# Relu and row mean on one core: 126 rows a partition between two blocks of 128 rows, and the last block's means stored turned, as four runs behind the main store

## The chip, the cores and the metric

The kernel runs on one core of one Trainium2 chip. The time is the device time of one execution in microseconds (us); medians are over several executions. A profile is a separate look at one execution, and its span is about 1.4 us shorter than the execution's time (161.59 us and 160.2 us for the profiled run of the kernel before).

In the text, DVE is VectorE, ACT is ScalarE, POOL is GpSimd and SP is SyncE, which issues the DMAs here.

## The reference

```python
batch, seq, dim = 32, 512, 1024
x = np.random.randn(batch, seq, dim).astype(np.float32)

def reference(x):
    relu_x = np.maximum(x, 0)
    return np.mean(relu_x, axis=-1).astype(np.float32)
```

These are 16,384 rows of 1024 numbers: 67.11 MB are read, 65,536 bytes written.

## The kernel before

The first 128 rows lie one to a partition. They are loaded ahead of all else, and their means are turned by a 32x32 transpose into four rows of 32, which are stored in mid-stream. The other 16,256 rows lie 127 to a partition (`J` after the subtraction): seven loads of 16 rows, then 7, 4, 2 and 1 rows, then the last row in pieces of columns. ACT and DVE take rows in turn; each pass is a relu with a running sum.

```python
xfirst, xmain = xf[:P, :], xf[P:, :]
outfirst, outmain = out.flatten()[:P], out.flatten()[P:]
J = J - 1
xr = xmain.rearrange("(p j) d -> p j d", p=P, j=J)
...
row_pieces = [7, 4, 2, 1]
col_pieces = [512, 256, 256]
...                      # the last row: ACT takes piece 1, DVE piece 2
nc.scalar.wait_ge(loaded[i + 1], 16)
act_row(nc, last[:, :512], last[:, D:D + 1]).then_inc(act, 1)
nc.vector.wait_ge(loaded[i + 2], 16)
dve_row(nc, last[:, 512:768], last[:, D + 1:D + 2]).then_inc(dve, 1)
nc.vector.wait_ge(act, n_done + 1)
nc.vector.wait_ge(dve, n_done + 1)
nc.vector.wait_ge(loaded[i + 3], 16)
nc.vector.scalar_tensor_tensor(      # piece 3, and the two sums that lie behind it
    out=last[:, 768:], in0=last[:, 768:], scalar=0.0, in1=scale[:, :], op0=ALU.max, op1=ALU.mult,
    accum_out=res[:, J - 1:J],
).then_inc(dve, 1)

nc.sync.wait_ge(pool, 2)
nc.sync.wait_ge(dve, n_done + 2)
nc.sync.dma_start(out=outr, in_=res[:, :]).then_inc(stored, 16)
```

The two partial sums of the last row lie in the columns right behind it, so the last instruction on DVE (called the **combining instruction** below) reduces the third piece and adds them in one go. The one store of 128 runs of 508 B follows it.

Of the kernel before, what the change touches and what calls it, by code (L numbers as in the profile page):

```python
# [8 lines left out]
ALU = mybir.AluOpType  # L9
# [3 lines left out]
def act_row(nc, src, acc):  # L13

    return nc.scalar.activation(out=src, in_=src, func=ACT.Relu, accum_out=acc)  # L15


def dve_row(nc, src, acc, init=None):

    return nc.vector.tensor_scalar(  # L20
        out=src, in0=src, scalar1=0.0, scalar2=init,
        op0=ALU.max, op1=ALU.add, accum_out=acc,
    )


def issue_ahead_of_entry_barrier(nc, n):


    entry = nc.cur_f.blocks[0].instructions
    for _ in range(n):  # L30
        body, load = next(
            (block.instructions, k)
            for block in nc.cur_f.blocks[1:]
            for k, ins in enumerate(block.instructions)
            if ins.opcode == "DMACopy"
        )
        first = body[load]
        assert first.engine == mybir.EngineType.SP and not first.sync_info.on_wait
        assert all(i.opcode in ("Drain", "EventSemaphore") or i.engine != first.engine for i in body[:load])
        del body[load]  # L40
        at = next(k for k, i in enumerate(entry) if i.engine == first.engine and i.opcode == "Drain")
        entry.insert(at, first)


@with_exitstack
def kernel(
    ctx: ExitStack,
    tc: tile.TileContext,
    x: bass.AP,
    out: bass.AP,  # L50
):


    tc.close()
    tc.compile()  # L55

    nc = tc.nc
    P = nc.NUM_PARTITIONS
    xf = x.flatten_outer_dims()
    R, D = xf.shape  # L60
    assert R % P == 0
    J = R // P
    inv = 1.0 / D

    xfirst, xmain = xf[:P, :], xf[P:, :]
    outfirst, outmain = out.flatten()[:P], out.flatten()[P:]
    J = J - 1
    xr = xmain.rearrange("(p j) d -> p j d", p=P, j=J)
    outr = outmain.rearrange("(p j) -> p j", p=P, j=J)

    NB = 16
    BUFS = 3
    full = J // NB

    row_pieces = [7, 4, 2, 1]
    assert full * NB + sum(row_pieces) + 1 == J
    col_pieces = [512, 256, 256]
    assert sum(col_pieces) == D

    def sbuf(name, *shape):  # L80
        return ctx.enter_context(nc.sbuf_tensor(name, list(shape), F32))

    bufs = [sbuf(f"rows{b}", P, NB, D) for b in range(BUFS)]
    sums, res, part = sbuf("sums", P, J), sbuf("res", P, J), sbuf("part", P, 2)


    last = sbuf("last", P, D + 2)
    scale = sbuf("scale", P, D // 4 + 2)

    row0, mean0, turned0 = sbuf("row0", P, D), sbuf("mean0", P, 32), sbuf("turned0", P, 32)  # L90


    loaded = [nc.alloc_semaphore(f"loaded{i}") for i in range(full + len(row_pieces) + len(col_pieces) + 1)]
    act, dve, pool = (nc.alloc_semaphore(n) for n in ("act", "dve", "pool"))
    first = nc.alloc_semaphore("first")
    stored = nc.alloc_semaphore("stored")



    hinted = (nc.scalar, nc.vector)  # L100
    flag = nc.alloc_registers("flag", engines=[e.engine for e in hinted])
    nc.regs_mov(flag, 1)
    nc.br("rows_begin", engines=mybir.ALL_ENGINES)
    body = ctx.enter_context(nc.body("rows_begin", valid_engines=mybir.ALL_ENGINES))
    hints = [e.mark_branch_hint_location() for e in hinted]


    def load(i, dst, src):
        nc.sync.dma_start(out=dst, in_=src).then_inc(loaded[i], 16)

    def buf_free(t):

        if t >= BUFS:
            nc.sync.wait_ge(act, t - BUFS + 1)
            nc.sync.wait_ge(dve, t - BUFS + 1)

    for t in range(full):
        buf_free(t)
        if t == 0:
            load(-1, row0[:, :], xfirst)  # L120
        load(t, bufs[t % BUFS][:, :, :], xr[:, t * NB:(t + 1) * NB, :])
        if t == BUFS:

            nc.sync.wait_ge(first, 2)
            nc.sync.dma_start(
                out=outfirst.rearrange("(q i) -> q i", i=32), in_=turned0[0:P:32, :],
            ).then_inc(stored, 16)
    j0 = full * NB
    buf_free(full)
    xt = bufs[full % BUFS]  # L130
    lo, i = 0, full
    for n in row_pieces:
        load(i, xt[:, lo:lo + n, :], xr[:, j0 + lo:j0 + lo + n, :])
        lo, i = lo + n, i + 1
    c = 0
    for w in col_pieces:
        load(i, last[:, c:c + w], xr[:, J - 1, c:c + w])
        c, i = c + w, i + 1


    nc.gpsimd.memset(mean0[:, :], 0.0)  # L141
    nc.gpsimd.memset(scale[:, :], inv).then_inc(pool, 1)  # L142

    def rows(i, xt, lo, n, j0):
        nc.scalar.wait_ge(loaded[i], 16)
        nc.vector.wait_ge(loaded[i], 16)
        for k in range(lo, lo + n):
            j = j0 + k
            done = (dve_row if j % 2 else act_row)(nc, xt[:, k, :], sums[:, j:j + 1])
            if k >= lo + n - 2:  # L150
                done.then_inc(dve if j % 2 else act, 1)

    def finish(after, lo, hi):

        nc.gpsimd.wait_ge(act, after)
        nc.gpsimd.wait_ge(dve, after)
        nc.gpsimd.tensor_scalar(  # L157
            out=res[:, lo:hi], in0=sums[:, lo:hi], scalar1=inv, scalar2=0.0, op0=ALU.mult, op1=ALU.add,
        )

    nc.scalar.wait_ge(pool, 1)
    nc.vector.wait_ge(pool, 1)
    nc.scalar.wait_ge(loaded[-1], 16)
    nc.scalar.activation(  # L164
        out=row0[:, :], in_=row0[:, :], func=ACT.Relu, scale=inv, accum_out=mean0[:, 0:1],
    ).then_inc(first, 1)
    nc.vector.wait_ge(first, 1)
    nc.vector.transpose(turned0[:, :], mean0[:, :]).then_inc(first, 1)  # L168
    for t in range(full):
        rows(t, bufs[t % BUFS], 0, NB, t * NB)  # L170
    finish(full, 0, j0)
    lo, i = 0, full
    for n in row_pieces[:-1]:
        rows(i, xt, lo, n, j0)
        lo, i = lo + n, i + 1
    finish(i, j0, j0 + lo)


    prev = xt[:, lo, :]
    nc.scalar.wait_ge(loaded[i], 16)  # L180
    act_row(nc, prev[:, :448], part[:, 0:1]).then_inc(act, 1)
    nc.vector.wait_ge(loaded[i], 16)
    dve_row(nc, prev[:, 448:], part[:, 1:2]).then_inc(dve, 1)
    n_done = i + 1
    nc.gpsimd.wait_ge(act, n_done)
    nc.gpsimd.wait_ge(dve, n_done)
    nc.gpsimd.tensor_scalar(  # L187
        out=res[:, J - 2:J - 1], in0=part[:, 0:1], scalar1=part[:, 1:2], scalar2=inv, op0=ALU.add, op1=ALU.mult,
    ).then_inc(pool, 1)
    nc.scalar.wait_ge(loaded[i + 1], 16)  # L190
    act_row(nc, last[:, :512], last[:, D:D + 1]).then_inc(act, 1)
    nc.vector.wait_ge(loaded[i + 2], 16)
    dve_row(nc, last[:, 512:768], last[:, D + 1:D + 2]).then_inc(dve, 1)
    nc.vector.wait_ge(act, n_done + 1)
    nc.vector.wait_ge(dve, n_done + 1)
    nc.vector.wait_ge(loaded[i + 3], 16)
    nc.vector.scalar_tensor_tensor(  # L197
        out=last[:, 768:], in0=last[:, 768:], scalar=0.0, in1=scale[:, :], op0=ALU.max, op1=ALU.mult,
        accum_out=res[:, J - 1:J],
    ).then_inc(dve, 1)  # L200


    nc.sync.wait_ge(pool, 2)
    nc.sync.wait_ge(dve, n_done + 2)
    nc.sync.dma_start(out=outr, in_=res[:, :]).then_inc(stored, 16)

    used = [s.num for s in (*loaded, act, dve, pool, first)]
    assert used == list(range(used[0], used[0] + len(used)))
    nc.sync.sem_clear(range(used[0], used[-1] + 1))
    nc.sync.wait_ge(stored, 32).then_inc(stored, -32)  # L210

    for e, hint in zip(hinted, hints):
        e.br_lt(flag, 1, on_true="rows_begin", on_false="rows_end").branch_hint(hint)
    nc.br("rows_end", engines=[e for e in mybir.ALL_ENGINES if e not in (h.engine for h in hinted)])
    nc.switch_bb("rows_end")

    issue_ahead_of_entry_barrier(nc, 2)
# [30 lines left out]
```

## Time and profile before

| What | Before |
|---|---|
| median (3 runs) | 161.53 us (161.3 to 161.62) |
| span of the profiled run | 160.2 us |
| DMA queue's packets, share of 16 engines' span | 97.7% |
| DVE, ACT busy | 46%, 44% |
| start of the passes over the last but one row (448 columns on ACT, 576 on DVE) | 156.49 us |
| combining instruction | 158.06 us |
| issue of the store | 158.57 us |
| end | 160.2 us |

The body is a stream of loads which nothing in the change makes smaller. So the useful reading of a change like this one is the **tail**: from the start of the passes over the last but one row to the end of the span. Before, it is 160.2 - 156.49 = 3.71 us. The end is given to a tenth, so a tail is good to about 0.05 us. The prediction shows the lines.

### The profile page before, as it was taken

The numbers are of one execution on the slowest core, as the hardware profiler recorded it, in microseconds if no ns is written. First come the engines' busy times: TensorE is split into PE (matmuls) and PEld (weight loads), VectorE is DVE, ScalarE is ACT, GpSimd is POOL, SyncE is SP. The second block draws the span as 40 slices with busy tenths as digits, with TensorE's granted clock in tenths as the row PEclk, the third lists the DMA queues.
The fourth block names the chain that finished last, engine by engine and source line by source line (L and its number), as shares of the span: only waits on it lengthen the run. The fifth ranks groups of instructions, "written<-read, shape, count | busy, mean of one in ns | idle before, by whom it ended". The sixth has DMA issues, their size and how long they took to land. (4 is left out here: it accounts for less than half of the span.)

```text
span 160.2 us, 347 instructions
## 1 busy us (share of the span) xinstructions
DVE 73.3 (46%) x131; ACT 70.4 (44%) x133; POOL 1.3 (1%) x9
## 2 busy tenths in 40 slices
DVE  0000029900498006960079500993009920299984
ACT  1400029800496006950079300991009900299983
POOL 1000000000000000000000000000000000000001
DMA  9969969979989899699699699699699797998992
GB/s 393 507 278 523 507 278 523 442 344 523 409 376 523 360 425 524 294 491 523 262 524 523 262 523 524 262 523 523 262 524 458 327 523 327 425 451 367 419 412 102
DMA packets 2312, 67.18 MB, mean 419 GB/s; under 512 B 392, under 2 KB 648, under 8 KB 1032
## 3 DMA queue, kind: packets, MB, share of 16 engines
q1 hardware_dynamic: 2312, 67.18, 97.7%
HBM read 67.11 MB, written 0.07 MB: 419 GB/s over the span
## 5 line engine op out<-in xcount | busy, mean ns | idle before, releaser
L20 DVE TENSOR_SCALAR_CACHE_REDUCE rows<-rows 128x1024 f32<-128x1024 f32 (+1 forms) x63 | 72.1, 1208 | 78.9 <-DMA rows<-in_x_dram 78.7
L15 ACT ACTIVATE rows<-rows 128x1024 f32<-128x1024 f32 x64 | 66.2, 1035 | 84.1 <-DMA rows<-in_x_dram 83.9
L15 ACT ACTIVATION_READ_ACCUMULATOR rows<-rows 128x1 f32 x64 | 11.9, 186 | 0.0
L20 DVE DVE_READ_ACCUMULATOR rows<-rows 128x1 f32 x63 | 5.2, 82 | 0.0
L168 DVE STREAM_TRANSPOSE turned<-mean 128x32 f32<-128x32 f32 x1 | 0.2, 213 | 5.9 <-ACT row L164 5.9
L164 ACT ACT_TABLE_LOAD x1 | 1.3, 1283 | 3.3 <-DMA row<-in_x_dram 3.3
L157 POOL TENSOR_SCALAR res<-sums 128x112 f32<-128x112 f32 (+1 forms) x2 | 0.5, 250 | 154.0 <-DVE rows L20 154.0
L164 ACT ACTIVATE row<-row 128x1024 f32<-128x1024 f32 x1 | 1.1, 1056 | 0.0
L15 ACT ACTIVATE last<-last 128x512 f32<-128x512 f32 x1 | 0.6, 630 | 0.0
L20 DVE TENSOR_SCALAR_CACHE_REDUCE last<-last 128x256 f32<-128x256 f32 x1 | 0.4, 420 | 0.3 <-DMA last<-in_x_dram 0.3
L197 DVE SCALAR_TENSOR_TENSOR last<-last,scale 128x258 f32<-128x258 f32 x1 | 0.4, 428 | 0.1
L142 POOL MEMSET scale<- 128x258 f32 x1 | 0.3, 314 | 0.0
L187 POOL TENSOR_SCALAR res<-part 128x1 f32<-128x1 f32 x1 | 0.3, 267 | 0.6 <-DVE rows L20 0.6
L164 ACT ACTIVATION_READ_ACCUMULATOR row<-row 128x1 f32 x1 | 0.2, 186 | 0.0
L15 ACT ACTIVATION_READ_ACCUMULATOR last<-last 128x1 f32 x1 | 0.2, 186 | 0.0
L141 POOL MEMSET mean<- 128x32 f32 x1 | 0.1, 126 | 1.5 <-POOLq L55 1.5
L232 POOL MEMSET const-uint8-127<- 128x1 uint8 x1 | 0.1, 103 | 0.0
L232 POOL MEMSET const-bfloat16-1.0<- 128x1 bf16 x1 | 0.1, 102 | 0.0
L232 POOL MEMSET const-float32-0.0<- 128x1 f32 x1 | 0.1, 99 | 0.2 <-issue 0.2
L232 POOL MEMSET const-float32-1.0<- 128x1 f32 x1 | 0.1, 99 | 0.0
L20 DVE DVE_READ_ACCUMULATOR last<-last 128x1 f32 x1 | 0.1, 83 | 0.0
L197 DVE DVE_READ_ACCUMULATOR last<-last,scale 128x1 f32 x1 | 0.1, 82 | 0.0
## 6 DMA issues: line engine op xcount, KB each, us to landing
rows<-in_x_dram SPq DMA_DIRECT2D x1, 3584.0 KB, 38.1
rows<-in_x_dram SPq DMA_DIRECT2D x1, 2048.0 KB, 42.6
rows<-in_x_dram SPq DMA_DIRECT2D x1, 1024.0 KB, 44.7
row<-in_x_dram SPq DMA_DIRECT2D x1, 512.0 KB, 3.3
rows<-in_x_dram SPq DMA_DIRECT2D x1, 512.0 KB, 45.4
last<-in_x_dram SPq DMA_DIRECT2D x1, 256.0 KB, 45.6
last<-in_x_dram SPq DMA_DIRECT2D x2, 128.0 KB, 45.4
rows<-in_x_dram SPq DMA_DIRECT2D x7, 48.8
```

The costliest lines, as they stand in the source:

```text
L15: return nc.scalar.activation(out=src, in_=src, func=ACT.Relu, accum_out=acc)
L20: return nc.vector.tensor_scalar(out=src, in0=src, scalar1=0.0, scalar2=init, op0=ALU.max, op1=ALU.add, accum_out=acc,)
L141: nc.gpsimd.memset(mean0[:, :], 0.0)
L142: nc.gpsimd.memset(scale[:, :], inv).then_inc(pool, 1)
L157: nc.gpsimd.tensor_scalar(out=res[:, lo:hi], in0=sums[:, lo:hi], scalar1=inv, scalar2=0.0, op0=ALU.mult, op1=ALU.add,)
L164: nc.scalar.activation(out=row0[:, :], in_=row0[:, :], func=ACT.Relu, scale=inv, accum_out=mean0[:, 0:1],).then_inc(first, 1)
L168: nc.vector.transpose(turned0[:, :], mean0[:, :]).then_inc(first, 1)
L187: nc.gpsimd.tensor_scalar(out=res[:, J - 2:J - 1], in0=part[:, 0:1], scalar1=part[:, 1:2], scalar2=inv, op0=ALU.add, op1=ALU.mult,).then_i ...
L197: nc.vector.scalar_tensor_tensor(out=last[:, 768:], in0=last[:, 768:], scalar=0.0, in1=scale[:, :], op0=ALU.max, op1=ALU.mult, accum_out=r ...
L232: nc = _bacc.Bacc("TRN2", target_bir_lowering=False, num_devices=1)
```

## The change

The intent: let the bulk of the results leave early, while the last row is still in work, and leave only a small store for the end. To get a small store with long runs, the last 128 rows become a block of their own, one to a partition, as the first 128 are; their means are turned by a transpose, which makes four runs of 128 B. The last row's columns are also split anew.

```diff
-    xfirst, xmain = xf[:P, :], xf[P:, :]
-    J = J - 1
+    xfirst, xmain, xlast = xf[:P, :], xf[P:-P, :], xf[-P:, :]
+    outfirst, outmain, outlast = outs[:P], outs[P:R - P], outs[R - P:]
+    J = J - 2
...
-    col_pieces = [512, 256, 256]
+    col_pieces = [576, 192, 256]
...
-    act_row(nc, last[:, :512], last[:, D:D + 1]).then_inc(act, 1)
+    act_row(nc, last[:, :448], last[:, D:D + 1]).then_inc(act, 1)
+    nc.vector.wait_ge(loaded[i + 1], 16)
+    dve_row(nc, last[:, 448:576], last[:, D + 1:D + 2])
     nc.vector.wait_ge(loaded[i + 2], 16)
-    dve_row(nc, last[:, 512:768], last[:, D + 1:D + 2]).then_inc(dve, 1)
+    dve_row(nc, last[:, 576:768], last[:, D + 2:D + 3]).then_inc(dve, 1)
...
-        accum_out=res[:, J - 1:J],
+        accum_out=mean1[:, 0:1],
     ).then_inc(dve, 1)
+    nc.vector.wait_ge(dve, n_done + 2)
+    nc.vector.transpose(turned1[:, :], mean1[:, :]).then_inc(dve, 1)

     nc.sync.wait_ge(pool, 2)
-    nc.sync.wait_ge(dve, n_done + 2)
     nc.sync.dma_start(out=outr, in_=res[:, :]).then_inc(stored, 16)
+    nc.sync.wait_ge(dve, n_done + 3)
+    store_turned(outlast, turned1)      # in_=turned1[0:P:32, :], 4 rows of 32
```

More of the change, by code (lines that the diff above doesn't have):

```diff
@@ L63 @@
     inv = 1.0 / D
-    xfirst, xmain = xf[:P, :], xf[P:, :]
-    outfirst, outmain = out.flatten()[:P], out.flatten()[P:]
-    J = J - 1
+    xfirst, xmain, xlast = xf[:P, :], xf[P:-P, :], xf[-P:, :]
+    outs = out.flatten()
+    outfirst, outmain, outlast = outs[:P], outs[P:R - P], outs[R - P:]
+    J = J - 2
     xr = xmain.rearrange("(p j) d -> p j d", p=P, j=J)
@@ L75 @@
     row_pieces = [7, 4, 2, 1]
-    assert full * NB + sum(row_pieces) + 1 == J
-    col_pieces = [512, 256, 256]
+    assert full * NB + sum(row_pieces) == J
+    col_pieces = [576, 192, 256]
     assert sum(col_pieces) == D
@@ L84 @@
     sums, res, part = sbuf("sums", P, J), sbuf("res", P, J), sbuf("part", P, 2)
-    last = sbuf("last", P, D + 2)
-    scale = sbuf("scale", P, D // 4 + 2)
+    last = sbuf("last", P, D + 3)
+    scale = sbuf("scale", P, D // 4 + 3)
     row0, mean0, turned0 = sbuf("row0", P, D), sbuf("mean0", P, 32), sbuf("turned0", P, 32)
+    mean1, turned1 = sbuf("mean1", P, 32), sbuf("turned1", P, 32)
     loaded = [nc.alloc_semaphore(f"loaded{i}") for i in range(full + len(row_pieces) + len(col_pieces) + 1)]
@@ L115, in buf_free, with store_turned @@
             nc.sync.wait_ge(dve, t - BUFS + 1)
+    def store_turned(dst, turned):
+        nc.sync.dma_start(
+            out=dst.rearrange("(q i) -> q i", i=32), in_=turned[0:P:32, :],
+        ).then_inc(stored, 16)
     for t in range(full):
@@ L124 @@
             nc.sync.wait_ge(first, 2)
-            nc.sync.dma_start(
-                out=outfirst.rearrange("(q i) -> q i", i=32), in_=turned0[0:P:32, :],
-            ).then_inc(stored, 16)
+            store_turned(outfirst, turned0)
     j0 = full * NB
@@ L136 @@
     for w in col_pieces:
-        load(i, last[:, c:c + w], xr[:, J - 1, c:c + w])
+        load(i, last[:, c:c + w], xlast[:, c:c + w])
         c, i = c + w, i + 1
     nc.gpsimd.memset(mean0[:, :], 0.0)
+    nc.gpsimd.memset(mean1[:, :], 0.0)
     nc.gpsimd.memset(scale[:, :], inv).then_inc(pool, 1)
@@ L187 @@
     nc.gpsimd.tensor_scalar(
-        out=res[:, J - 2:J - 1], in0=part[:, 0:1], scalar1=part[:, 1:2], scalar2=inv, op0=ALU.add, op1=ALU.mult,
+        out=res[:, J - 1:J], in0=part[:, 0:1], scalar1=part[:, 1:2], scalar2=inv, op0=ALU.add, op1=ALU.mult,
     ).then_inc(pool, 1)
     nc.scalar.wait_ge(loaded[i + 1], 16)
-    act_row(nc, last[:, :512], last[:, D:D + 1]).then_inc(act, 1)
+    act_row(nc, last[:, :448], last[:, D:D + 1]).then_inc(act, 1)
+    nc.vector.wait_ge(loaded[i + 1], 16)
+    dve_row(nc, last[:, 448:576], last[:, D + 1:D + 2])
     nc.vector.wait_ge(loaded[i + 2], 16)
-    dve_row(nc, last[:, 512:768], last[:, D + 1:D + 2]).then_inc(dve, 1)
-    nc.vector.wait_ge(act, n_done + 1)
+    dve_row(nc, last[:, 576:768], last[:, D + 2:D + 3]).then_inc(dve, 1)
     nc.vector.wait_ge(dve, n_done + 1)
     nc.vector.wait_ge(loaded[i + 3], 16)
+    nc.vector.wait_ge(act, n_done + 1)
     nc.vector.scalar_tensor_tensor(
         out=last[:, 768:], in0=last[:, 768:], scalar=0.0, in1=scale[:, :], op0=ALU.max, op1=ALU.mult,
-        accum_out=res[:, J - 1:J],
+        accum_out=mean1[:, 0:1],
     ).then_inc(dve, 1)
+    nc.vector.wait_ge(dve, n_done + 2)
+    nc.vector.transpose(turned1[:, :], mean1[:, :]).then_inc(dve, 1)
     nc.sync.wait_ge(pool, 2)
-    nc.sync.wait_ge(dve, n_done + 2)
     nc.sync.dma_start(out=outr, in_=res[:, :]).then_inc(stored, 16)
+    nc.sync.wait_ge(dve, n_done + 3)
+    store_turned(outlast, turned1)
     used = [s.num for s in (*loaded, act, dve, pool, first)]
@@ L209 @@
     nc.sync.sem_clear(range(used[0], used[-1] + 1))
-    nc.sync.wait_ge(stored, 32).then_inc(stored, -32)
+    nc.sync.wait_ge(stored, 48).then_inc(stored, -48)
     for e, hint in zip(hinted, hints):
```

## The prediction

> **What bounds the kernel now.** I read the page's header and slices first, then the SP queue's own waits, then the order of time from 156 us on, and last the DMA view of the final microsecond.
>
> The page (third line: mean busy share of the 16 DMA engines in 40 slices; last line: one group of part 5, with busy time, mean ns, idle time before it and what ended it):
>
> ```profile
> span 160.2 us, 347 instructions
> DVE 73.3 (46%) x131; ACT 70.4 (44%) x133; POOL 1.3 (1%) x9
> DMA  9969969979989899699699699699699797998992
> q1 hardware_dynamic: 2312, 67.18, 97.7%
> L20 DVE TENSOR_SCALAR_CACHE_REDUCE rows<-rows 128x1024 f32<-128x1024 f32 (+1 forms) x63 | 72.1, 1208 | 78.9 <-DMA rows<-in_x_dram 78.7
> ```
>
> Neither compute engine is busy half of the time, and nearly all their idle time ends on a load. The DMA queue is busy 97.7% of the span: the body is the stream of 67.11 MB. The change moves the same 67.11 MB in and the same 65,536 bytes out, so the body can change only if the stream's rate does. What is left is the tail.
>
> The tail in order of time (start, duration, engine, line, operation; in brackets the idle time and its releaser; L15 is ACT's row helper, L20 that of DVE, L197 the last combining instruction, L205 the main store):
>
> ```profile
> 156.49 0.58 ACT L15 ACTIVATE rows<-rows 128x448 f32<-128x448 f32 x1
> 156.49 0.75 DVE L20 TENSOR_SCALAR_CACHE_REDUCE rows<-rows 128x576 f32<-128x576 f32 x1
> ...
> 157.16 0.63 ACT L15 ACTIVATE last<-last 128x512 f32<-128x512 f32 x1
> 157.17 0.08 DVE L20 DVE_READ_ACCUMULATOR rows<-rows 128x1 f32 x1
> 157.42 0.27 POOL L187 TENSOR_SCALAR res<-part 128x1 f32<-128x1 f32 x1 [0.63 <-DVE rows L20]
> 157.54 0.42 DVE L20 TENSOR_SCALAR_CACHE_REDUCE last<-last 128x256 f32<-128x256 f32 x1 [0.29 <-DMA last<-in_x_dram]
> 157.70 0.19 ACT L15 ACTIVATION_READ_ACCUMULATOR last<-last 128x1 f32 x1
> 157.89 0.08 DVE L20 DVE_READ_ACCUMULATOR last<-last 128x1 f32 x1
> 158.06 0.43 DVE L197 SCALAR_TENSOR_TENSOR last<-last,scale 128x258 f32<-128x258 f32 x1
> 158.41 0.08 DVE L197 DVE_READ_ACCUMULATOR last<-last,scale 128x1 f32 x1
> 158.57 0.35 SPq L205 DMA_DIRECT2D out_dram<-res  x1
> ```
>
> The end is a chain: second piece of the last row lands (157.54), DVE reduces it (to 157.97), 0.09 us of waiting, the combining instruction (158.06 to 158.50), 0.07 us until the store is issued (158.57), then 1.63 us until the span ends at 160.2. The view of the queue's own waits has the last part (line waited at, releaser, total, times, longest):
>
> ```profile
> SPq L204 <- DVE last L197: 45.6, 1, 45.6
> SPq L210 <- SPq L210: 1.2, 1, 1.2
> ```
>
> So 1.2 us are the wait for the store's completion. The DMA view cut to 159.3 to 159.9 (40 slices of 15 ns) splits it:
>
> ```profile
> DMA  0000000144475999999997864352010000000000
> DMA packets 144, 0.07 MB, mean 108 GB/s; under 512 B 144, under 2 KB 144, under 8 KB 144
> ```
>
> The first packet starts at slice 7, that is 159.41, or 0.84 us after the issue; the last ends at slice 30, 159.75. They are 128 data packets and 16 more, nine to each engine if spread evenly, in 0.34 us, so 0.038 us each. From the last packet to the span's end are 0.45 us.
>
> **What the skill says.** (1) The Trainium skill, "Perfetto Trace Analysis", section "DMA Instruction — HWDGE (DVE, Sync)": the reported DMA instruction covers issuing only, and the final descriptor updates the semaphore after the write before it is confirmed, a delay that can be long towards HBM. The trace agrees: 0.35 us of instruction, but 1.63 us to the end, 0.45 of them after the last packet. (2) "DMA: Bandwidth & Descriptors", section "Why a DMA increments its semaphore by 16 and not by 1": a DMA from SP runs on the largest number of engines up to 16 that divides the slowest dimension, and the sequencer writes the missing increments itself. The turned store has 4 runs, so 4 engines and 12 increments. This fits its issue of 632 ns, at 32.7 us, against 348 ns for the 128-row store; no run yet isolates it. (3) The same page, section "Latency and other measured facts": copies slow down at row pitches of large powers of two (207 GB/s at 512 KiB, 103 at 4 MiB, 214 when padded). Here the pitch of a partition goes from 127 x 4 = 508 KiB to 126 x 4 = 504 KiB; neither is a power of two, and the stream before holds 429 GB/s between 20 and 140 us. (4) "VectorE: DVE Perf Modes", section "The DRAIN you can't avoid": a read of a result on the same engine needs a semaphore to be safe. The added turn waits on its own engine's semaphore; the same kind of wait cost 0.09 us in the chain above.
>
> **The change part by part.** *Loads.* Same bytes; the seven big loads keep their sizes and the last row keeps three pieces, of 576, 192 and 256 columns for 512, 256 and 256. The sum of the first two is unchanged, so the second should still land near 157.5. The first landed about 157.1 (issued at 111.5, 45.6 to landing) and has 64 x 4 x 128 = 32.8 KB more; at the 383 GB/s seen between 156 and 157 us that is 0.09 us, so some 157.2. The third landed about 157.8 (issued at 112.5, 45.3) and was not waited for. Sum: 0.
>
> *Last row, ACT.* 448 columns for 512. The 448-column pass above took 0.67 us from its start to the end of its accumulator read (156.49 to 157.16), the 512-column one 0.73 (157.16 to 157.89). From 157.22 that is 157.89 again.
>
> *Last row, DVE.* The durations 1.215, 0.754 and 0.420 us for 1024, 576 and 256 columns lie on 0.157 + 0.00103 per column. The added 128 columns take 0.29 us (157.22 to 157.51), within the 0.29 us in which DVE had idled. The 192 columns take 0.355 instead of 0.42, from 157.54 to 157.90: 0.07 earlier. The combining instruction starts at about 157.99, and its accumulator read ends at 158.42 instead of 158.50. Sum: -0.07, rounded.
>
> *The turn.* Added on the path: 0.09 wait plus the 0.213 us that the same instruction took at 5.9 us, 0.30 in all. It ends at 158.73; 0.07 later, at 158.80, the last store is issued. That is 0.23 later than before (158.80 - 158.57).
>
> *Main store.* It leaves when POOL has the last column, 157.69 + 0.07 = 157.76, 0.81 us earlier; with 1.63 us it is complete at 159.39, before the last store's first packets. It leaves the path.
>
> *Last store.* 4 data packets of 128 B, on four engines one each and one for the semaphore: 2 instead of 9, so 7 x 0.038 = 0.27 us less of packet time, if the rest (0.84 before, 0.45 after) stays. 1.63 - 0.27 = 1.36, and the span ends at 158.80 + 1.36 = 160.16. The longer issue (0.63 us) ends at 159.43, before the packets, and is hidden.
>
> *Head and the rest.* One more memset of 0.13 us on POOL ends near 2.4 us, while ACT waits for the first load until 3.35: nothing. Packets: 8 more (4 data, 4 semaphore), so 2320.
>
> **Sum:** -0.07 + 0.30 - 0.27 = -0.04 us, on a median of 161.53: **161.5**. In effect nothing: what the turn puts on the path, the small store gives back.
>
> **Rivals.** *A: the store's cost is latency, not packets.* If its 1.63 us is the round trip whatever the count, the saving of 0.27 falls away, and the time is +0.23, 161.8. For it: 0.84 + 0.45 of the 1.63 us have no packet in them. Against: the 0.34 us of packets are real, and fewer must show. It may still show by half, since a single packet has its write confirmed before the semaphore's with nothing to overlap it. *B: the store of four runs is slow to start*, its packets leaving only after the 12 increments: 0.28 us more (0.632 - 0.348), together with A 162.0. The old one's packets can't be told among the loads around 33 us. *C: the pitch changes the stream.* One per cent of rate would be 1.6 us, many times all else; 429 GB/s in mid-stream, the same in the first and the later buffers within some per cent, speaks against a limit set by the addresses, but the trace has only one pitch. It could go either way: 161.5 ± 0.8 for half a per cent. *D: the last row as one contiguous block of 512 KB* could move faster or slower than one scattered at 508 KiB; the rate there is 383 GB/s against 429. If it rose to 429 the last 512 KB would come 0.15 us sooner, and DVE's wait shrink by as much: 161.35.
>
> **Range and chances.** A and B give up to 0.5 on the slow side, C and D both ways a few tenths, and the three runs before spread over 0.32 us. I take **161.0 to 162.1**. Two per cent is 3.2 us: only C could reach it, and would need a stream slower or faster by 2%. Faster 0.01, same 0.98, slower 0.01.
>
> **What would show it right or wrong.** In the profile after: the main store issued near 157.8 and the last one near 158.8; a second transpose of about 0.21 us just before it; its issue about 0.63 us; a handful of packets near 159.65 and the end about 0.45 after them; a 128-column DVE pass of about 0.29 us with less than 0.1 us of idle after it; 2320 packets at 97 to 98%. Wrong is the size of the store's saving if the end is over 1.5 us after the last issue; wrong is the claim on the stream if the last prev-row passes (156.49 before) start over 0.4 us earlier or later.

## The result and the profile after

The changed kernel takes 161.59 us in the median (161.36 to 162.11, 6 runs), the kernel before 161.47 us in the same rounds (161.3 to 161.75, 6 runs). A ratio here is the mean time of one kernel's runs over that of the other's in the same rounds, so it is not quite the ratio of the medians: 1.0008, with a 95% interval of 0.9989 to 1.0026. By the threshold of 2% it is the same.

The page of the changed kernel (span; busy time of the engines; DMA share in 40 slices; the DMA queue with packets, MB and share):

```profile
span 160.2 us, 351 instructions
DVE 73.7 (46%) x134; ACT 70.3 (44%) x133; POOL 1.4 (1%) x10
DMA  9969979979989899699699699699699699599992
q1 hardware_dynamic: 2320, 67.18, 97.6%
```

The same span, the same stream, 8 packets more, as forecast. But equal spans do not mean equal tails. The tail of the changed kernel in order of time (start, duration, engine, line, operation; in brackets idle time and releaser; L214 is the main store, L121 the turned one):

```profile
156.27 0.58 ACT L15 ACTIVATE rows<-rows 128x448 f32<-128x448 f32 x1
...
157.05 0.29 DVE L20 TENSOR_SCALAR_CACHE_REDUCE last<-last 128x128 f32<-128x128 f32 x1
157.05 0.58 ACT L15 ACTIVATE last<-last 128x448 f32<-128x448 f32 x1
157.33 0.35 DVE L20 TENSOR_SCALAR_CACHE_REDUCE last<-last 128x192 f32<-128x192 f32 x1
157.50 0.35 SPq L214 DMA_DIRECT2D out_dram<-res  x1
157.53 0.18 ACT L15 ACTIVATION_READ_ACCUMULATOR last<-last 128x1 f32 x1
157.85 0.43 DVE L205 SCALAR_TENSOR_TENSOR last<-last,scale 128x259 f32<-128x259 f32 x1 [0.15 <-ACT last L15]
158.20 0.08 DVE L205 DVE_READ_ACCUMULATOR last<-last,scale 128x1 f32 x1
158.32 0.21 DVE L210 STREAM_TRANSPOSE turned<-mean 128x32 f32<-128x32 f32 x1
158.56 0.54 SPq L121 DMA_DIRECT2D out_dram<-turned  x1
```

In this execution the stream ran out 0.22 us earlier (156.27 against 156.49), and the tail took 160.2 - 156.27 = 3.93 us, 0.22 us longer than before; the two cancel. The main store does leave early. The combining instruction has the same place in the tail (1.58 us after its start, 1.57 before) and has idled 0.15 us for ACT. From its end to the last issue are 0.28 us instead of 0.07: the turn. And the last store, small as it is, takes 160.2 - 158.56 = 1.64 us to the end, as long as the large one took before (1.63).

The DMA view of the changed kernel from 159.3 to 160.2 (40 slices of 22.5 ns) shows where:

```profile
DMA  0000000000000000000100000000000000000000
GB/s 0 0 0 0 0 0 0 0 0 0 0 0 0 0 0 0 0 0 0 12 6 6 0 0 0 0 0 0 0 0 0 0 0 0 0 0 0 0 0 0
```

The few packets start in slice 19, at 159.73, which is 1.17 us after the issue; in the kernel before, the first packet came 0.84 us after it. The packets saved 0.27 us and the later start took 0.33.

### The profile page after: what moved, and what is told of

Its sections match the earlier page's. It is cut to its first block, busy times and chain, and to the rows that moved or that the text cites. A ratio compares the mean times of both kernels' runs of the same rounds, so it can differ in the third digit from the quotient of the medians.

```text
span 160.2 us, 351 instructions
## 1 busy us (share of the span) xinstructions
DVE 73.7 (46%) x134; ACT 70.3 (44%) x133; POOL 1.4 (1%) x10
## 4 chain that ended last, share of the span: by engine, by line
DMA 84%; DVE 12%; SPq 1%; issue 1%; ACT 0%; DVEq 0%
DMA rows<-in_x_dram 56%; DMA last<-in_x_dram 28%; DVE rows L20 12%; SPq L111 1%; DVE last L205 0%; ACT last L15 0%; DVE turned L210 0%; DVEq L204 0%; SPq L117 0%
## 5 line engine op out<-in xcount | busy, mean ns | idle before, releaser
L20 DVE TENSOR_SCALAR_CACHE_REDUCE last<-last 128x128 f32<-128x128 f32 (+1 forms) x2 | 0.6, 320 | 0.0
L15 ACT ACTIVATE last<-last 128x448 f32<-128x448 f32 x1 | 0.6, 577 | 0.1
```

The source lines that it names most:

```text
L15: return nc.scalar.activation(out=src, in_=src, func=ACT.Relu, accum_out=acc)
L20: return nc.vector.tensor_scalar(out=src, in0=src, scalar1=0.0, scalar2=init, op0=ALU.max, op1=ALU.add, accum_out=acc,)
```

## The experiments

Theory: the change lengthens the tail by about 0.2 us. The turn adds that much, and the four-run store saves nothing since it starts late. Rivals: the early main store is not off the path; the new row pitch changes the stream; the late start comes from the four engines, as the prediction's rival B had it, or from following the main store.

The edits are shown as cuts: what only follows from them (the widths of buffers, the count that the last wait on `stored` expects) is left out. This is the tail of every kernel that ran, from its timeline. All columns but the first are in us, counted from the start of the passes over the last but one row; "store" is the end less the last issue. The two ladders go on after the end, and have no place in the table.

| Kernel | Passes start at | Combining | Last issue | End | Store |
|---|---|---|---|---|---|
| before | 156.49 | 1.57 | 2.08 | 3.71 | 1.63 |
| before, again | 156.22 | 1.59 | 2.09 | 3.68 | 1.59 |
| changed | 156.27 | 1.58 | 2.29 | 3.93 | 1.64 |
| changed, again | 156.72 | 1.57 | 2.28 | 3.88 | 1.60 |
| column | 156.26 | 1.57 | 2.03 | 9.34 | 7.31 |
| unturned4 (wrong) | 156.63 | 1.56 | 2.03 | 3.57 | 1.54 |
| old_pieces | 156.16 | 1.56 | 2.27 | 3.84 | 1.57 |
| swapped | 156.81 | 1.57 | 2.91 | 4.59 | 1.68 |
| consecutive4 (wrong) | 156.71 | 1.57 | 2.29 | 3.49 | 1.20 |
| two_queues (last of four issues, on ACT) | 156.29 | 1.56 | 2.84 | 4.01 | 1.17 |
| last_columns | 156.26 | 1.55 | 2.01 | 3.54 | 1.53 |
| balanced | 156.54 | 1.49 | 1.96 | 3.46 | 1.50 |

### Both kernels again: after_again and before_again

No edit but a comment.

> The changed kernel once more, to see what repeats. If the tail is what the change lengthened: about 3.93 us from the start of the 448/576-column passes to the end again, the last store's first packet about 1.17 us after its issue again. If the earlier end of the stream (passes starting at 156.27 against 156.49 before) was luck, their start moves about by 0.2 us; if it comes from the new row pitch, it stays near 156.27. Time against the kernel before: between +0.0 and +0.3 us.

> The kernel before once more. If the change lengthened the tail and the rest is luck of the stream, its tail from the start of the 448/576-column passes to the end is 3.71 us again, within 0.05, while these passes start anywhere from 156.2 to 156.8. If the old row pitch were slower, they would start at 156.5 or later, and those of the changed layout (156.27, 156.26, 156.22, 156.63, 156.72 so far) earlier on the whole. Ratio to the kernel before 1.000, and the interval shows what two equal kernels give.

The changed kernel: 161.81 us (6 runs) against 161.36 (11), ratio 1.002 (1.0006 to 1.0034). The kernel before against itself: 161.34 us (5) against 161.34 (9), ratio 0.9991 (0.9977 to 1.0005). The tails repeat to 0.05 us: 3.93 and 3.88 for the changed kernel, 3.71 and 3.68 for the one before. The passes' start does not: 156.27 and 156.72, 156.49 and 156.22. So the earlier end of the stream in the first profile was luck. The last store's first packet comes 1.17 us after its issue in both profiles of the changed kernel. Kernels with the new pitch start between 156.16 and 156.81, those with the old one between 156.22 and 156.54. No effect of the pitch is seen, though these profiles could not show one of 0.1 us. The change costs about 0.2 us of tail, which the second set of rounds resolves (0.2% of 161 us is 0.32 us) and the first does not.

### The turn: unturned4

```diff
-    nc.vector.wait_ge(dve, n_done + 2)
-    nc.vector.transpose(turned1[:, :], mean1[:, :]).then_inc(dve, 1)
...
-    nc.sync.wait_ge(dve, n_done + 3)
-    store_turned(outlast, turned1)
+    nc.sync.wait_ge(dve, n_done + 2)
+    store_turned(outlast, mean1)
```

> Without the turn: the last store takes 4 rows of the unturned tile, so the last 128 results are wrong on purpose. Theory (the turn lies wholly on the path): the last store's issue comes 0.07 us after the combining instruction's accumulator read instead of 0.28, and the tail from the start of the 448/576-column passes is 3.93 - 0.21 = 3.72 us; the store still takes about 1.64 us from issue to end. Rival (the turn is partly hidden, as the store's end waits for something else, such as the main store): the tail stays above 3.85 us.

The results were wrong. The issue comes 2.03 us into the tail instead of 2.29, and the tail is 3.57 us. The expectation was 3.72; the rest lies in an issue 0.04 us after the accumulator read instead of 0.07 and in a store 0.1 us shorter, which the rounding of the ends may account for. The turn lies wholly on the path and costs about 0.25 us. The rival falls.

### Without a turn, right: column

```diff
-    nc.sync.wait_ge(dve, n_done + 3)
-    store_turned(outlast, turned1)
+    nc.sync.wait_ge(dve, n_done + 2)
+    nc.sync.dma_start(out=outlast.rearrange("(p o) -> p o", o=1), in_=mean1[:, 0:1]).then_inc(stored, 16)
```

with the transpose taken out.

> The last store taken straight from the column, 128 runs of 4 B on 16 engines, no turn; the result stays right. Theory (a store costs what its start-up and its count of packets cost; the 4-run form starts 0.33 us later than a 128-row form, 1.17 against 0.84 us from issue to first packet): the first packet comes 0.84 us after the issue, the end about 1.6 after it, and the issue about 0.07 us after the combining instruction instead of 0.28; so the tail from the start of the last 448/576-column passes to the end is 3.93 - 0.21 = 3.7 us, as in the kernel before. Rival (the 4-run form saves by its few packets, as the prediction had it): the column is slower from issue to end than the 4-run form's 1.64 us. Second rival (runs of 4 B cost much more each than 508 B): first to last packet well over 0.34 us. Time: 161.4 under the theory, within 0.3 us of both kernels.

166.83 us (5 runs), ratio 1.0335 (1.032 to 1.0351): 5.4 us slower. My expectation missed badly. Its theory had the beginning right: the issue was early (2.03 us), and the first packet came 0.85 us after it (0.84 expected). The packets were not slow either, against the second rival. The store is slower than the 4-run form's 1.64 us, as the first rival had it, but its count of packets is not the reason, as the ladders will show. The wait for the stores is what grew; first its line among the queue's own waits (line, releaser, total, times, longest), then the DMA view from 158.5 to 160.5 (40 slices of 50 ns, the end of the main store first, then the column):

```profile
SPq L219 <- SPq L219: 6.8, 1, 6.8
```

```profile
DMA  9620000000000543000000000000000000000000
```

The column's packets are over by 159.3, and its completion comes at 165.6. 128 runs of 4 B side by side are 512 bytes of output: the packets are over soon, but the completion comes 6.3 us after the last of them. What happens in these 6.3 us the trace does not show. For a block of rows that lie one to a partition, the turn is worth its 0.25 us.

### What the store's start depends on: ladder and ladder2

Each store by itself. After the two stores of the changed kernel, 24 (30 in the second) more follow, each behind a wait for the one before; the last of them makes the output right again.

```diff
+    for _ in range(3):
+        for dst, held in forms:
+            nc.sync.wait_ge(stored, done)
+            nc.sync.dma_start(out=dst, in_=held).then_inc(stored, 16)
+            done += 16
```

> After the two stores, 24 more, each waiting for the one before to complete, three times over: a column of 128 runs of 4 B; 16, 8, 4, 2 and 1 runs of 32 B; the main store of 128 runs of 504 B; 4 runs of 128 B. The last of them mends what the others wrote. Theory (few engines: the sequencer writes the missing increments, and the start of the packets is late with them): the issue instruction is 0.35 us for 128 and 16 runs and grows to about 0.54 at 4 runs and more at 2 and 1, and the time from issue to completion is longer at 4 runs of 32 B than at 16 runs of 32 B, by some 0.3 us. Rival (the late start came from following the main store by one us, or from the queue's state): alone, 4 runs start as soon as 16, 0.84 us after the issue, and complete in about 1.35 us. Packet count: 128 runs complete 0.2 to 0.3 us later than 16 runs.

> The first ladder showed that 16 runs on 16 engines start as late as 4 on 4 (issue 0.54 us, first packet 1.17 us after it), so the number of engines is not the cause; 128 unspaced rows and a single row start early. Now, three times over, each waiting for the one before: 128 runs of 8 B at spaced addresses; 4 runs of 128 B from four consecutive partitions and from partitions 32 apart; 16 runs of 32 B from consecutive partitions and from partitions 8 apart; 64 runs of 8 B from consecutive partitions and from every second; 2 consecutive rows; 1 row; 4 runs 32 apart to mend the output. Theory (the step between the partitions of the source makes the issue long and the start late): consecutive rows issue in about 0.34 us and complete in 1.25 to 1.35 us, the stepped ones in 0.54 and 1.6 to 1.7, for each pair. Rival (any number of rows below 128 and above one is slow): both of a pair alike, 0.5 and 1.6. For the column's 7 us: if its runs of 4 B are slow because they lie in the same few hundred bytes of the output, the spaced runs of 8 B complete in about 1.6 us; if short runs are slow wherever they lie, they take about 7 us too.

The ladder's stores in order of time (start, duration of the issue, line, what; the group of five is 16, 8, 4, 2 and 1 runs of 32 B); as each waits for the one before, the distance between two starts is the time from issue to completion:

```profile
160.08 0.34 SPq L229 DMA_DIRECT2D out_dram<-mean  x1
167.53 6.62 SPq L229 DMA_DIRECT2D out_dram<-turned  x5
174.94 0.35 SPq L229 DMA_DIRECT2D out_dram<-res  x1
176.90 0.54 SPq L229 DMA_DIRECT2D out_dram<-turned  x1
```

In the second ladder the pair that matters, 4 consecutive rows (first line) and 4 rows 32 partitions apart (second), and then the store after them, all from the timeline in short cuts:

```profile
161.78 0.29 SPq L228 DMA_DIRECT2D out_dram<-turned  x1
162.94 0.52 SPq L228 DMA_DIRECT2D out_dram<-turned  x1
164.52 0.33 SPq L228 DMA_DIRECT2D out_dram<-turned  x1
```

162.94 - 161.78 = 1.16 us for consecutive rows, 164.52 - 162.94 = 1.58 for stepped ones. All forms, three times each or more (the last store of each ladder, 1.61 and 1.63 us, ends at a rounded span and is left out):

| Store | Issue, us | Issue to completion, us |
|---|---|---|
| 128 runs of 504 B (main) | 0.34 to 0.35 | 1.59, 1.78, 1.96 |
| 128 runs of 4 B, side by side | 0.33 to 0.34 | 6.83 to 7.45 |
| 128 runs of 8 B, 504 B apart | 0.34 to 0.35 | 1.41 to 1.43 |
| 64 runs of 8 B, side by side, consecutive or every second partition | 0.49 to 0.51 | 3.46 to 4.08 |
| 16 runs of 32 B, consecutive | 0.32 to 0.33 | 1.30 to 1.32 |
| 16 runs of 32 B, 8 partitions apart | 0.53 to 0.55 | 1.67 to 1.71 |
| 8 runs of 32 B, 16 apart | 0.58 to 0.60 | 1.62 to 1.64 |
| 4 runs of 32 B, 32 apart | 0.51 to 0.52 | 1.54 to 1.55 |
| 2 runs of 32 B, 64 apart | 0.49 to 0.50 | 1.47 to 1.48 |
| 4 runs of 128 B, consecutive | 0.25 to 0.29 | 1.13 to 1.16 |
| 4 runs of 128 B, 32 apart | 0.52 to 0.55 | 1.58 to 1.60 |
| 2 runs of 128 B, consecutive | 0.24 to 0.25 | 1.07 |
| 1 run of 32 or 128 B | 0.23 to 0.27 | 1.05 to 1.06 |

The first ladder refuted its own theory. 16 runs on 16 engines start as late as 4 on 4: their first packet comes 1.17 us after the issue, though with 16 engines (32 packets, 16 of data and 16 of semaphores) no increment is missing. A single row, with 15 increments missing, issues as fast as any. Following the main store is not it either: 4 stepped runs took 1.58 to 1.60 us with nothing ahead of them. The second ladder has the cause for 4 and for 16 rows: a step between the source's partitions adds about 0.25 us to the issue and 0.4 us to the completion (1.16 against 1.58; 1.31 against 1.69). For the 4 rows all of that lies before the first packet, which comes 0.75 us after the issue without the step and 1.17 with it. Among unstepped stores of one shape, fewer runs do complete sooner, as the prediction held, though only by about 0.1 us (4, 2 and 1 runs of 128 B: 1.14, 1.07 and 1.05). What stays open: the pair of 64 rows went as the rival had it. The consecutive ones issue in 0.50 us and send their first packet at 1.15 us, though they have no step, so a step is not the only thing that delays a start, and why it delays one was not looked into.

The column's 7 us come from short runs lying side by side: the same number of runs of 8 B, 504 B apart, completes in 1.42 us. The width, 8 B for 4, does not explain it: 64 runs of 8 B side by side take 3.46 us and more.

### The cause in place: consecutive4

```diff
-    store_turned(outlast, turned1)      # in_=turned1[0:P:32, :]
+    nc.sync.dma_start(
+        out=outlast.rearrange("(q i) -> q i", i=32), in_=turned1[0:4, :],
+    ).then_inc(stored, 16)
```

> The changed kernel with the last store's four rows taken from partitions 0 to 3 instead of 0, 32, 64 and 96; the last 128 results are mostly wrong on purpose. All else is as changed, the turn too. Theory (the step between the source's partitions is what the last store lost by; in the second ladder 4 consecutive rows completed in 1.13 to 1.16 us, 4 stepped ones in 1.58 to 1.60): issue about 0.27 us, end 1.15 to 1.2 after it, tail from the start of the 448/576-column passes 3.45 to 3.5 us instead of 3.9, time 0.2 us below the kernel before (ratio about 0.999) and 0.4 below the changed one. Rival (in place, behind the main store, the end waits for something else): tail 3.8 or more.

The results were wrong. 161.13 us (6 runs) against 161.45 (11), ratio 0.9974 (0.9957 to 0.9991, which is 0.15 to 0.7 us); tail 3.49 us, within what was expected. Its last issue:

```profile
159.00 0.30 SPq L216 DMA_DIRECT2D out_dram<-turned  x1
```

From there to the end at 160.2 are 1.20 us instead of 1.60 to 1.64, and to the first packet 0.76 us instead of 1.17. With this one edit the tail is 0.4 us shorter than the changed kernel's and 0.2 shorter than the one before's: for these four rows the step is the whole of what the last store lost, and the small store would have paid for its turn.

### The early main store: swapped

```diff
     nc.sync.wait_ge(pool, 2)
-    nc.sync.dma_start(out=outr, in_=res[:, :]).then_inc(stored, 16)
     nc.sync.wait_ge(dve, n_done + 3)
     store_turned(outlast, turned1)
+    nc.sync.dma_start(out=outr, in_=res[:, :]).then_inc(stored, 16)
```

> The changed kernel with the turned store first and the main store behind it, so that the main store is the last again. Theory (sending the main store early takes it off the path, but gains only what it had cost): the turned store is issued at the same place in the tail, its issue of 0.54 us holds the main store back, the end comes 0.54 + 0.05 + 1.63 = 2.2 us after the turned store's issue instead of 1.64, the tail is 4.5 us, the time 162.2. The turned store's first packet still comes about 1.17 us after its issue though nothing is ahead of it in the queue.

One run, 162.78 us, tail 4.59 us (4.5 expected). The end comes 2.26 us after the turned store's issue. So in the changed kernel the early main store is off the path; put last, it costs 0.7 us. The turned store's first packet is at 160.30, 1.16 us after its issue at 159.14, with nothing ahead of it.

### The split of the last row: old_pieces

```diff
-    col_pieces = [576, 192, 256]
+    col_pieces = [512, 256, 256]
...
-    act_row(nc, last[:, :448], last[:, D:D + 1]).then_inc(act, 1)
-    nc.vector.wait_ge(loaded[i + 1], 16)
-    dve_row(nc, last[:, 448:576], last[:, D + 1:D + 2])
+    act_row(nc, last[:, :512], last[:, D:D + 1]).then_inc(act, 1)
```

> The changed kernel with the last row in pieces of 512, 256 and 256 columns again, as in the kernel before; layout, turn and stores as changed. Theory (the new split gains nothing, as ACT now waits for the larger first piece): from the start of the 448/576-column passes to the start of the combining instruction 1.57 us, as with the new split, and the tail 3.9 us. Rival (the new split gains the 0.07 us that the prediction gave it): 1.65 us and 4.0 us.

161.49 us (4 runs) against 161.34 (9), ratio 1.0011 (0.9991 to 1.0031). The combining instruction starts 1.56 us into the tail, with the new split at 1.57 or 1.58. The new split gains nothing.

### Repairs: two_queues, last_columns, balanced

First, four single rows, which have no step, two issued by SP and two by ACT:

```diff
-    nc.sync.wait_ge(dve, n_done + 3)
-    store_turned(outlast, turned1)
+    for e, quarters in ((nc.sync, (0, 1)), (nc.scalar, (2, 3))):
+        e.wait_ge(dve, n_done + 3)
+        for q in quarters:
+            e.dma_start(out=outlast[32 * q:32 * q + 32].rearrange("(q i) -> q i", i=32),
+                        in_=turned1[32 * q:32 * q + 1, :]).then_inc(stored, 16)
```

> The changed kernel with the last store as four single rows, two issued by SP and two by ACT, so that no source has a step; the result is right. By the ladders a single row issues in 0.25 us and completes in 1.05, so the second one on each queue completes at about 0.3 + 1.06 = 1.36 us, 0.22 before the stepped store: tail 3.65 to 3.7, like the kernel before, ratio 0.999 to 1.001. If issues of the two engines hold each other up, about 1.6 us and a tail of 3.9.

161.63 us (4 runs) against 161.45 (11), ratio 1.0004 (0.9982 to 1.0027); tail 4.01 us. SP's two issues took 0.27 and 0.25 us, as a single row does alone, but ACT's first took 0.51 us beside them, so its second began only at 159.13, and the end came 1.17 us after that. No gain. Whether SP's issues held ACT's up, or ACT's first issue is slow by itself, no run shows.

Then the kernel before, with its one store cut: all columns but two early, the last two after the combining instruction. There is no turn, and the runs are 508 B apart.

```diff
     nc.sync.wait_ge(pool, 2)
+    nc.sync.dma_start(out=outr[:, :J - 2], in_=res[:, :J - 2]).then_inc(stored, 16)
     nc.sync.wait_ge(dve, n_done + 2)
-    nc.sync.dma_start(out=outr, in_=res[:, :]).then_inc(stored, 16)
+    nc.sync.dma_start(out=outr[:, J - 2:], in_=res[:, J - 2:]).then_inc(stored, 16)
```

> The kernel before with its one store cut in two: all columns but the last two as soon as POOL is done, and the last two columns, 128 runs of 8 B spaced 508 B apart, after the combining instruction; no turn, no new layout. By the second ladder such spaced runs complete in 1.41 to 1.43 us, against 1.63 for the 128 runs of 508 B at the end of the kernel before: tail 3.5 us instead of 3.7, ratio about 0.999. If writing beside bytes that the main store still has in flight is slow, as in the column at 4 B apart, the tail is far over 4 us.

Right results; 161.23 us (6 runs) against 161.45 (11), ratio 0.9986 (0.9966 to 1.0006); tail 3.54 us, so the store of 8 B runs took 1.53 us here, 0.1 more than alone.

Last, the same with the new pieces and less for ACT, which the combining instruction had waited for:

```diff
-    col_pieces = [512, 256, 256]
+    col_pieces = [576, 192, 256]
...
-    act_row(nc, last[:, :512], last[:, D:D + 1]).then_inc(act, 1)
+    act_row(nc, last[:, :384], last[:, D:D + 1]).then_inc(act, 1)
+    nc.vector.wait_ge(loaded[i + 1], 16)
+    dve_row(nc, last[:, 384:576], last[:, D + 1:D + 2])
```

> The kernel before with the store cut in two as in the last run, and the changed kernel's pieces of 576, 192 and 256 columns, of which ACT takes 384 columns and DVE 192 and 192. In the changed kernel the combining instruction waited 0.15 us for ACT's 448 columns, while DVE was done; 64 columns fewer take about 0.05 us from ACT. Expected: combining instruction 1.50 to 1.53 us after the start of the 448/576-column passes instead of 1.55 to 1.58, tail 3.45 to 3.5 us against 3.54 of the run with the cut store alone, ratio to the kernel before about 0.998, not clearly apart from that run. Rival (the first piece's landing or the semaphore between ACT and DVE sets it): no change of the tail.

Right results; 161.16 us (5 runs) against 161.32 (9), ratio 0.9986 (0.9972 to 1.0). The combining instruction starts at 1.49 us instead of 1.55, and the tail is 3.46 us, the shortest of all that are right: 0.2 us below the kernel before and 0.4 below the changed one. By the profile it beats both kernels; by the clock the lead over the kernel before is at the edge of what five rounds resolve.

## Why the prediction was right or wrong

The time was right (161.5 forecast, 161.59 measured, range 161.0 to 162.1), and so was the reason for the range: only the tail changes, and by tenths. Its sum was not: it had -0.04 us, the tails say +0.2. That the median came so near is partly luck, as the first rounds could not tell the two apart. And its conclusion, that the small store gives back what the turn costs, does not hold for this store. By its own steps, with its times counted from 156.49, its start of the passes:

- **Loads, sum 0:** right. The stream is as before within its luck, the first piece let ACT start 0.78 us into the tail (0.73 forecast), and the second did not hold DVE. (The 0.05 us by which the first piece was late is the 0.05 by which ACT ends late in the next point.)
- **Last row, -0.07:** wrong by 0.08. DVE was done as forecast (1.42 us; forecast 1.41). But the combining instruction started at 1.58 instead of 1.50, as ACT, put down as level with DVE, ended at 1.45 (forecast 1.40) and DVE went on 0.13 us after it, not 0.09. That the wait on ACT was what held it is shown by the balanced run: with 64 columns fewer on ACT it started at 1.49.
- **The turn, +0.30:** right in place, too large by 0.09. The turn waited 0.04 us after the combining instruction and not 0.09, and the store was issued 0.03 us after the turn and not 0.07. The turn itself takes 0.21 us as forecast, all of it on the path.
- **Main store off the path:** right, at 1.23 us (forecast 1.27); the swapped run shows it from the other side.
- **Last store, -0.27:** this is the step that failed. "If the rest (0.84 before, 0.45 after) stays": the 0.45 about stayed (0.4), the 0.84 became 1.17, and the store took 1.60 to 1.64 us where 1.36 was forecast, over the 1.5 us that the prediction itself had named as the sign that the saving was wrong. The mechanism held (few packets take less time, and consecutive4's store took 1.20 us in place), but a source of every 32nd partition starts later, and that ate it. Its issue took 0.54 us, not the 0.63 taken over from the turned store in mid-stream, where it took 0.63 again.
- **Rival B** had the size nearly right (0.28 us more) and the cause wrong. I read the 632 ns of the old turned store as the cost of the 12 missing increments; four consecutive rows have the same 12 missing and issue in 0.25 to 0.29 us.
- **Rivals C and D**, pitch and block: not seen. With the new block and the old pieces (old_pieces) DVE started the second piece 1.07 us into the tail; in the two profiles of the kernel before it was 1.05 and 1.07.
- **Rival A**, a round trip that does not care for the count, had the number, +0.23 us, but by chance: consecutive4's 1.20 us show that the small store does save when its source has no step.

Corrected with the means of the two profiles of each kernel (the last store took 1.62 us, 0.26 more than forecast), the sum is -0.04 + 0.08 - 0.09 + 0.26 = +0.21 us, which is what their tails show.

## What to carry to other kernels

A last store's cost is the time from its issue to its completion, and it depends on its access patterns more than on its bytes: here a step between the source's partitions cost 0.4 us (4 and 16 rows), and 4 B runs side by side cost over 5 us. Before reshaping results to make the last store small, measure the very form of store by itself, in a chain where each waits for the one before. And when a change touches only the end of a long stream, compare tails from a common event, not spans, for the stream's own luck is as large as the effect.

## What the Trainium skill lacked or had wrong

- "DMA: Bandwidth & Descriptors", section "Why a DMA increments its semaphore by 16 and not by 1": it says that the sequencer writes the missing increments and gives no cost, which led me to blame them. No cost is seen: a single row with 15 missing issues in 0.23 to 0.27 us, 16 consecutive rows with none missing in 0.32 to 0.33.
- The same page has no word on what a step between the partitions of an SBUF source costs: 4 runs of 128 B complete in 1.13 to 1.16 us from consecutive partitions, in 1.58 to 1.60 from every 32nd; the issue takes 0.25 to 0.29 and 0.52 to 0.55 us.
- The same page, section "Latency and other measured facts", gives a first byte after about 600 ns; here the first packet starts 0.75 us after the issue of a store of four consecutive rows, 0.84 us after that of a 128-row store and 1.17 us after that of a stepped one.
- The same page warns of runs under 512 B, but not that their place decides: 128 runs of 4 B side by side complete in 6.83 to 7.45 us, 128 runs of 8 B 504 B apart in 1.41 to 1.43.
- "VectorE: DVE Perf Modes", section "The DRAIN you can't avoid", has a semaphore make such a read safe, and measured that it costs nothing extra in a chain of eight copies; in the short chain here 0.04 us passed between the combining instruction and the turn that waits for it.
